# RWKV recurrence on one Trainium2 core: each head keeps one half of the partitions, and its products become pairs in diagonal quadrants

## The chip, the cores and the metric

One core of a Trainium2 chip runs the kernel, a whole network of four layers on 256 tokens of width 1024. The metric is device time in microseconds (us). The engines are TensorE (PE in the views; its weight loads are PEld), VectorE (DVE), ScalarE (ACT), GpSimd (POOL) and SyncE (SP).

## What is computed

The four layers have three kinds of mixer: RWKV (layers 0 and 3), a selective state space (layer 1), attention in a sliding window (layer 2); feed-forward blocks stand around them. The change concerns RWKV. There, 16 heads of 64 each keep a 64x64 state, which is carried over the tokens:

```python
    def step(state, inp):
        r_t, w_t, k_t, v_t, kk_t, a_t = inp
        sa = jnp.einsum('bhvk,bhk->bhv', state, -kk_t)
        state = (state * w_t[:, :, None, :]
                 + sa[..., None] * (kk_t * a_t)[:, :, None, :]
                 + v_t[..., None] * k_t[:, :, None, :])
        return state, jnp.einsum('bhvk,bhk->bhv', state, r_t)

    _, y = lax.scan(step, state0, (tm(rh), tm(wh), tm(kh), tm(vh), tm(kk), tm(ah)))
```

Then y is normalised by head, a bonus `sum(r k r_k) v` is added, and the sum is multiplied by a gate and projected by `w_o`. Inputs and results are fp32.

## The kernel before

Activations lie transposed: 1024 channels are 8 tiles k of 128 partitions, each with 256 tokens along the free axis. A tile holds two heads, one in partitions 0 to 63 and one in 64 to 127 (`H2` is the pair of slices).

The recurrence is computed in 4 chunks c of 64 tokens. Within a chunk the dependence between tokens is a triangular system: its block products L (`pd`, L832) go to DRAM and come back with one 32x32 block in a partition (`dL`, then `LT`), are inverted there by 31 steps on VectorE (`solve`, L866 and L867), and go back by DRAM (`dTU`) into `U` and `T11`. `inverse` (L948, L953) completes the 64x64 inverses from the 32x32 blocks by small products. What remains for each chunk and tile is `recur`: 

- p1 (L1008, L1011): state times decayed directions, plus the masked products `GM` times the values; ScalarE copies it to r1.
- p3 (L1016): the inverse U times r1; ScalarE copies it into UV.
- p4 (L1021): the new state out of keys and values, one product of 128 rows with [K|Aa] as weights; VectorE scales it into ST (L1026, L1028), once for each head.
- py (L1033, L1035): the chunk's output.

Where things lie: of tiles 0 to 3 the solved rows (U, r1, the upper part of UV) are in the upper half of the partitions, of tiles 4 to 7 in the lower half (`half = k // 4`), for both heads of a tile side by side along the free axis; the values are in the other half. So p4 sums over keys times values and directions times solved rows in a single product of 128 rows. `AK` keeps K and Aa side by side for that, by chunk. The state of two heads, ST, is a 128x128 tile whose off-diagonal blocks are zero.

The stages of one RWKV layer: projections and low-rank products; then for pairs of tiles `directions`, `decay`, `factors` (which makes pd), with `grams` (L933, masked on VectorE by L934) and `tokens` (four transposes, L965) of tiles 0 to 3; then `solve` with the values' projection (`whole`, L694) beside it; then the stage in which four lanes run `inverse` and `recur`, lane n for tiles n and n+4, with `grams`, `tokens`, `bonus` (L986), `inverse` of tiles 4 to 7, the rest of `whole`, and `close` (L1050 normalisation, `pgt` gate) woven between them. The output projection `pjrwo` (`mm3`, L381 to L383) follows, from Y in the order of k.

The generators are woven turn by turn into one program, and a scheduler in the framework then places the instructions on each engine, so the order is not that of the code. On an engine instructions run in their order. A pool tag "q" of QB buffers holds r1 and old; the mamba layer borrows one for its `Bt`.

An fp32 product is one instruction in the order of the program and two passes in the trace; an fp32r product is one pass. `mm` writes PSUM; `pc` is one PSUM tile for each tile k.

Of the kernel before, what the change touches and what calls it, by code (L numbers as in the profile page):

```python
# [23 lines left out]
QB = 8  # L24
# [226 lines left out]
class Net:  # L251
# [400 lines left out]
    def rwkv(self, l, j):  # L652
# [106 lines left out]


        AK = [self.b8("AK", F32, (P, 4, 4, 2, 64)) for _ in range(2)]
        Aa = lambda k, n=1: AK[k // 4][:, k % 4:k % 4 + n, :, k // 4].rearrange("p k c t -> p (k c) t")
        K = lambda k, n=1: AK[k // 4][:, k % 4:k % 4 + n, :, 1 - k // 4].rearrange("p k c t -> p (k c) t")
        keys = project(1, xk, lambda i, ps: act(K(i), c8(ps), AF.Copy))
# [9 lines left out]
        dL = self.dp.tile([2, 4, KT, 2, 32, 32], F32, name=f"dL_{l}")  # L774
# [4 lines left out]
        def directions(k0):  # L779

            sq = b2("sq")
            for d in range(2):
                act(c8(pair(sq)[:, d]), K(k0 + d), AF.Square, scale=self.p(f"k_k{j}", k0 + d))
            yield
            ss = self.ax("ss")
            mm(ss, blk, sq, start=True, stop=True)
            act(sq, ss, AF.Relu, bias=self.eps[:, 2:3])
            act(sq, sq, AF.Ln, bias=self.eps[:, 3:4])
            act(sq, sq, AF.Exp, scale=-0.5)
            for d in range(2):  # L790
                V.scalar_tensor_tensor(c8(KK[:, k0 + d]), K(k0 + d), self.p(f"k_k{j}", k0 + d), c8(pair(sq)[:, d]), MUL, MUL)
            yield
# [21 lines left out]
        def factors(k0):  # L814
            ks = range(k0, k0 + 2)
            sl = slice(k0, k0 + 2)
            kt_, a_, ip, kk = K(k0, 2), Aa(k0, 2), c8(flat(IP[:, sl])), c8(flat(KK[:, sl]))
            ka = b2("ka")
            for d, k in enumerate(ks):
                act(c8(pair(ka)[:, d]), Aa(k), AF.Identity, scale=self.p(f"k_a{j}", k), bias=rest[:, k:k + 1])  # L820
            V.tensor_tensor(a_, a_, kk, MUL)
            V.tensor_tensor(a_, a_, ip, MUL)
            V.tensor_tensor(kt_, kt_, c8(ka), MUL)
# [4 lines left out]
            for d, k in enumerate(ks):  # L828
                for c in range(4):
                    f = slice(64 * c, 64 * c + 64)  # L830
                    for r in H2:
                        mm(pd[r, 256 * d + 64 * c:256 * d + 64 * c + 64], Aa(k)[r, c], SG[r, k, f], start=True, stop=True)  # L832
# [11 lines left out]
        def solve():  # L844
# [56 lines left out]
        lows, ups = [lora_wa(lwa)], [lora_up("wa2", (j,), P, lwa, [(H2[0], f"w0{j}", lambda k: c8(SG[:, k])), (H2[1], f"a0{j}", Aa)])]  # L901
# [10 lines left out]
        received, solved, ready, U, GMs, UVs, bos = set(), [], set(), [], {}, {}, {}  # L912
# [9 lines left out]
        gm = bc(C["gm"][:, None, :], [P, 4, P])  # L922

        def grams(k):

            while k not in received or k not in factored:
                yield
            if k // 2 not in GMs:
                GMs[k // 2] = self.b8("GM", F32, (P, 2, 8, P))
            for h_, r in enumerate(H2):  # L930
                pg = self.ax("pg")
                for c in range(4):
                    mm(pg[:, P * c:P * c + P], AK[k // 4][r, k % 4, c].rearrange("p q t -> p (q t)"), SR[r, :, k, 64 * c:64 * c + 64], start=True, stop=True)  # L933
                V.tensor_tensor(GMs[k // 2][:, k % 2, 4 * h_:4 * h_ + 4], pg.rearrange("p (u t) -> p u t", t=P), gm, MUL)  # L934
                yield

        ahead = lambda k0: chain(directions(k0), decay(k0), factors(k0))
        def inverse(k):
# [3 lines left out]
            p0, n = 64 * (k // 4), 2 * (k % 4)  # L942
            a, b = slice(p0, p0 + 32), slice(p0 + 32, p0 + 64)
            GM = GMs[k // 2][:, k % 2]
            at = lambda u: 8 * (u % 4) + n + u // 4
            px, x = self.ax("px"), self.b1("X2")
            for u in range(8):
                mm(px[b, 32 * u:32 * u + 32], GM[a, u, 32:64], U[1][a, at(u)], start=True, stop=True)  # L948
            act(x[b], px[b, :256], AF.Copy)
            yield  # L950
            pt = self.ax("pt")
            for u in range(8):
                mm(pt[a, 32 * u:32 * u + 32], x[b, 32 * u:32 * u + 32], U[0][b, at(u), 32:], start=True, stop=True)  # L953
            act(U[0][a].rearrange("p (c g) t -> p c g t", g=8)[:, :, n:n + 2, 32:], pt[a, :256].rearrange("p (h c t) -> p c h t", c=4, h=2), AF.Copy)
            ready.add(k)
            yield

        def tokens(k):

            rk = self.b1("rk")  # L960
            V.scalar_tensor_tensor(c8(rk), c8(R[:, k]), self.p(f"r_k{j}", k), K(k), MUL, MUL)
            pt = self.ax("tok")
            both = AK[k // 4][:, k % 4].rearrange("p c q t -> p (c q t)")
            for c in range(4):
                nc.tensor.transpose(pt[:, P * c:P * c + P], both[:, P * c:P * c + P], ident)  # L965
            act(both, pt, AF.Copy)
# [8 lines left out]
        def bonus(k):  # L975

            half = k // 4
            top, bot = H2[half], H2[1 - half]
            while k not in valued:
                yield  # L980
            if half not in UVs:
# [846 lines left out]
```

## Time and profile before

| what | value |
|---|---|
| runs (us) | 3042.39, 3039.34, 3040.65 |
| median | 3040.65 |
| profiled execution, its own time | 3042.72 |
| its span in the profile | 3040.9 |
| PE busy | 2907.3 (96%) |
| DVE busy | 2176.8 (72%) |
| ACT busy | 1557.4 (51%) |
| stage of the recurrence, layer 0 | 358.20 to 494.30 in the span |
| stage of the recurrence, layer 3 | 2163.00 to 2304.30 in the span |

The profiled execution lies 2.07 us above the median, and 1.82 us of its time lie outside its span. A stage of the recurrence is taken here from the first product that needs the solved blocks (px, L948) to the last product of `recur` (L1033, L1035).

### The profile page before, as it was taken

The numbers are of one execution on the slowest core, as the hardware profiler recorded it, in microseconds if no ns is written. First come the engines' busy times: TensorE is split into PE (matmuls) and PEld (weight loads), VectorE is DVE, ScalarE is ACT, GpSimd is POOL, SyncE is SP. The second block draws the span as 40 slices with busy tenths as digits, with TensorE's granted clock in tenths as the row PEclk, the third lists the DMA queues.
The fourth block names the chain that finished last, engine by engine and source line by source line (L and its number), as shares of the span: only waits on it lengthen the run. The fifth ranks groups of instructions, "written<-read, shape, count | busy, mean of one in ns | idle before, by whom it ended". The sixth has DMA issues, their size and how long they took to land. (4 is left out here: it accounts for less than half of the span.)

```text
span 3040.9 us, 57272 instructions
## 1 busy us (share of the span) xinstructions
PE 2907.3 (96%) x23002; PEld 2740.7 (90%) x23002; DVE 2176.8 (72%) x3805; ACT 1557.4 (51%) x2713; POOL 88.9 (3%) x115
## 2 busy tenths in 40 slices
PE   7999899999998999999999999999899999999998
PEld 6997678999997989999988999987778999889898
DVE  8886434888787888878887888775526757566754
ACT  5446234545556765455575445445234546644543
POOL 0001200000001100000000000002100000000000
PEclk9999888999999999999999999999878999999999
DMA  9983313797874547888945887853404665544564
GB/s 320 329 312 92 117 36 112 266 308 261 292 268 151 163 154 226 289 281 280 317 132 163 304 305 253 297 173 96 127 18 125 208 181 179 177 144 125 160 184 129
DMA packets 184220, 612.33 MB, mean 201 GB/s; under 512 B 30929, under 2 KB 33361, under 8 KB 183954
## 3 DMA queue, kind: packets, MB, share of 16 engines
q1 hardware_dynamic: 168626, 595.49, 60.0%
q0 software_dynamic: 3744, 9.24, 1.0%
q10 hardware_dynamic: 11584, 3.93, 0.6%
q8 instruction: 180, 2.95, 0.4%
q14 instruction: 86, 0.70, 0.1%
HBM read 603.31 MB, written 5.28 MB: 200 GB/s over the span
## 5 line engine op out<-in xcount | busy, mean ns | idle before, releaser
L294 ACT ACTIVATE wh<-raw 128x1024 fp32r<-128x1024 f32 (+3 forms) x824 | 851.1, 1036 | 955.5 <-DMA raw<-in_wi 286.5
L373 DVE TENSOR_TENSOR wl<-raw,wh 128x1024 fp32r<-128x1024 f32 (+3 forms) x824 | 987.3, 1200 | 400.5 <-ACT wh L294 393.0
L382 PE MATMUL pjwi<-xl,wh 128*128 128x256 f32 x2568 | 720.8, 282 | 4.5 <-DVE xl L506 4.1
L383 PE MATMUL pjwi<-xh,wl 128*128 128x256 f32 x2568 | 717.4, 281 | 0.0
L381 PE MATMUL pjwi<-xh,wh 128*128 128x256 f32 x2568 | 714.5, 282 | 2.2 <-ACT sa L294 1.3
L382 PEld LDWEIGHTS pjwi<-xl,wh 128*128 128x128 f32 x2568 | 484.3, 189 | 7.2 <-DVE xl L506 6.9
L383 PEld LDWEIGHTS pjwi<-xh,wl 128*128 128x128 f32 x2568 | 483.3, 189 | 0.0
L381 PEld LDWEIGHTS pjwi<-xh,wh 128*128 128x128 f32 x2568 | 480.7, 189 | 2.8 <-ACT sa L294 1.6
L382 PE MATMUL pdwo<-gl,wh 128*128 128x256 f32 x1408 | 395.7, 281 | 0.0
L383 PE MATMUL pdwo<-gh,wl 128*128 128x256 f32 x1408 | 394.9, 280 | 0.0
L381 PE MATMUL pdwo<-gh,wh 128*128 128x256 f32 x1408 | 394.8, 280 | 0.0
L422 DVE SCALAR_TENSOR_TENSOR aring<-aring,cbc 128x1024 f32<-128x1024 f32 x286 | 343.5, 1219 | 4.1 <-DMA aring<-in_adaw 4.1
L383 PEld LDWEIGHTS pdwo<-gh,wl 128*128 128x128 f32 x1408 | 265.4, 188 | 0.0
L381 PEld LDWEIGHTS pdwo<-gh,wh 128*128 128x128 f32 x1408 | 265.1, 188 | 0.0
L382 PEld LDWEIGHTS pdwo<-gl,wh 128*128 128x128 f32 x1408 | 265.1, 188 | 0.0
L694 PE MATMUL whole<-mf,raw 128*128 128x256 f32 x512 | 127.0, 403 | 1.4 <-DMA raw<-in_rkv 1.4
L694 PEld LDWEIGHTS whole<-mf,raw 128*128 128x128 f32 x512 | 100.8, 201 | 22.6 <-issue 5.7
L383 PE MATMUL pjw2i<-xh,wl 128*128 128x256 f32 x416 | 119.0, 286 | 0.0
L381 PE MATMUL pjw2i<-xh,wh 128*128 128x256 f32 x416 | 118.5, 285 | 0.0
L382 PE MATMUL pjw2i<-xl,wh 128*128 128x256 f32 x416 | 117.9, 284 | 0.0
L381 PE MATMUL pjmbi<-xh,wh 128*128 128x256 f32 x352 | 101.1, 291 | 7.4 <-DVE cv L1152 4.9
L382 PE MATMUL pjmbi<-xl,wh 128*128 128x256 f32 x352 | 102.0, 291 | 0.1
(528 smaller groups left out, 5743.8 us busy)
## 6 DMA issues: line engine op xcount, KB each, us to landing
raw<-in_wi SPq DMA_DIRECT2D x352, 512.0 KB, 4.7
aring<-in_adaw SPq DMA_DIRECT2D x286, 512.0 KB, 5.4
raw<-in_wo SPq DMA_DIRECT2D x128, 512.0 KB, 4.8
raw<-in_w2i SPq DMA_DIRECT2D x56, 512.0 KB, 4.0
raw<-in_wo SPq DMA_DIRECT2D x64, 384.0 KB, 4.4
raw<-in_rkv SPq DMA_DIRECT2D x48, 512.0 KB, 3.7
raw<-in_mbi SPq DMA_DIRECT2D x48, 512.0 KB, 3.7
raw<-in_fg SPq DMA_DIRECT2D x22, 512.0 KB, 3.8
```

The costliest lines, as they stand in the source:

```text
L294: ins = self.nc.scalar.activation(out, in_, func, **k)
L373: self.last = self.nc.vector.tensor_tensor(lo, src, hi.bitcast(F32), SUB)
L381: mm(out, a, xh[:parts, k, :], start=start, stop=False)
L382: mm(out, a, xl[:parts, k, :], start=False, stop=False)
L383: mm(out, b, xh[:parts, k, :], start=False, stop=stop)
L422: ins = nc.vector.scalar_tensor_tensor(raw, raw, 1.0, self.cbc, MUL, MUL, accum_out=m[:, b % 24:b % 24 + 1])
L694: mm(ps[:, :T], w[:, k * P:k * P + P], x[0][:, k, :], start=k == 0, stop=k == KT - 1)
```

## The change

Each head stays in its own half of the partitions throughout. K and Aa become plain tiles; the values, transposed, go into `Vt`, the solved rows into `uu`, each head's 64 rows in its half. Every product of `recur` becomes a pair: 64x64 weights and 64 moving columns for the head in the upper half, the same for the lower one (`both`). What was one product of 128 rows for p4 is now two pairs that add up in PSUM, and the output gets a third pair (`uu` by `MB`), as p1 and py lose the rows of the other half. The state is one tile of 128x64, so that VectorE scales it in one instruction and no zeros are kept.

`grams` makes K against both directions (`pk`, masked into LM), and Aa against R alone (`pa`, masked into MB); Aa against the directions, which it had made again, is now kept from pd as LL and used in `inverse`. `tokens` and `bonus` transpose head by head, by products with a 64x64 block of the identity or of `cen`. `inverse` takes a pair of tiles at a time, both heads in two strips of rows. Four DMAs a pair of tiles write dL in place of eight; `solve` loads LT when all 8 tiles are there, where it loaded a half after 4. `recur` also waits until Vt is written (`prepared`). In the mamba layer Bt moves to a tile of its own, since "q" buffers are now 128x64 and 16 in number.

```diff
-QB = 8
+QB = 16
...
-        AK = [self.b8("AK", F32, (P, 4, 4, 2, 64)) for _ in range(2)]
...
+        K, Aa = self.b8("K"), self.b8("Aa")
+        LL = self.b8("LL")
...
-            tm = b2("tm")
-            act(tm, pd, AF.Copy)
+            act(flat(LL[:, sl]), pd, AF.Copy)
             for n in range(4):
                 h_, i = divmod(n, 2)
-                for d, k in enumerate(ks):
-                    queues[(n + d) % 2].dma_start(dL[k // 4, :, 2 * (k % 4) + h_, i].rearrange("c s t -> s c t"),
-                                                  c8(pair(tm)[32 * n:32 * n + 32, d])[:, :, 32 * i:32 * i + 32])
+                queues[n % 2].dma_start(dL[h_, k0:k0 + 2, :, i].rearrange("k c s t -> s (k c) t"),
+                                        c8(flat(LL[32 * n:32 * n + 32, sl]))[:, :, 32 * i:32 * i + 32])
...
-            for half in range(2):
-                while len(factored) < 4 * half + 4:
-                    yield
-                queues[half].dma_start(L[64 * half:64 * half + 64], dL[half].rearrange("c g i s t -> (c g i) (s t)"))
+            while len(factored) < KT:
+                yield
+            for h_ in range(2):
+                queues[h_].dma_start(L[64 * h_:64 * h_ + 64], dL[h_].rearrange("k c i s t -> (k c i) (s t)"))
...
-            for h_, r in enumerate(H2):
-                pg = self.ax("pg")
+            pa, pk = self.ax("pa"), self.ax("pk")
+            for c in range(4):
+                f = slice(64 * c, 64 * c + 64)
+                for r in H2:
+                    mm(pk[r, P * c:P * c + P], K[r, k, f], SR[r, :, k, f], start=True, stop=True)
+            V.tensor_tensor(LM[k // 4][:, k % 4], pk.rearrange("p (c t) -> p c t", c=4), bc(C["gm"][:, None, :], [P, 4, P]), MUL)
+            yield
+            for c in range(4):
+                f = slice(64 * c, 64 * c + 64)
+                for r in H2:
+                    mm(pa[r, f], Aa[r, k, f], R[r, k, f], start=True, stop=True)
+            V.tensor_tensor(c8(MB[0][:, k]), c8(pa[:, :T]), bc(C["gm"][:, None, 64:], [P, 4, 64]), MUL)
...
+            for n, u in xs:
+                k, c = divmod(u, 4)
+                for a, b in zip(lo, hi):
+                    mm(px[b, 32 * n:32 * n + 32], LL[a, k, 64 * c + 32:64 * c + 64], U[1][a, u], start=True, stop=True)
+            for b in hi:
+                act(x[b], px[b, :256], AF.Copy)
...
-                nc.tensor.transpose(pt[:, P * c:P * c + P], both[:, P * c:P * c + P], ident)
-            act(both, pt, AF.Copy)
+                    f = slice(64 * c, 64 * c + 64)
+                    for r in H2:
+                        mm(pt[r, o + 64 * c:o + 64 * c + 64], src[r, k, f], ident[r, r], start=True, stop=True)
+            for o, src in ((0, Aa), (T, K)):
+                act(src[:, k], pt[:, o:o + T], AF.Copy)
...
+            both = lambda out, w, x, **k: [mm(out[r], w[r], x[r], **k) for r in H2]
+            q1 = lambda name: self.sp.tile([P, 64], F32, tag="q", name=name, bufs=QB)
...
+                both(p1, lm[:, c, :64], V_[:, k, f], start=True, stop=not c)
                 if c:
-                    mm(p1, SR[:, 0, k, f], st, start=True, stop=False)
-
-                for h_ in range(2):
-                    mm(hc(p1, h_), GM[:, 4 * h_ + c, :64], uv(h_), start=not c, stop=not c or h_ == 1)
+                    both(p1, SR[:, 0, k, f], st, start=False, stop=True)
                 r1 = q1("r1")
-                act(r1[top], p1, AF.Copy)
-                yield
-                for h_ in range(2):
-                    mm(hc(p3, h_), U[0][top, 8 * c + n + h_], hc(r1[top], h_), start=True, stop=True)
-                act(UV[top, P * c:P * c + P], p3, AF.Copy)
+                act(r1, p1, AF.Copy)
+                yield
+                both(p3, U[0][:, 4 * k + c], r1, start=True, stop=True)
+                uu = q1("uu")
+                act(uu, p3, AF.Copy)
...
-                    mm(p4, both[:, P * c:P * c + P], UV[:, P * c:P * c + P], start=True, stop=True)
...
+                    both(p4, K[:, k, f], V_[:, k, f], start=True, stop=False)
+                    both(p4, Aa[:, k, f], uu, start=False, stop=True)
+                    new = q1("st")
...
-                for h_, r in enumerate(H2):
-                    mm(py[r, f], uv(h_), GM[:, 4 * h_ + c, 64:], start=True, stop=not c)
+                both(py[:, f], V_[:, k, f], lm[:, c, 64:], start=True, stop=False)
                 if c:
-                    mm(py[:, f], st, SR[:, 1, k, f], start=False, stop=True)
+                    both(py[:, f], st, SR[:, 1, k, f], start=False, stop=False)
+                both(py[:, f], uu, MB[0][:, k, f], start=False, stop=True)
...
-        lanes = [chain(repeat(None, s), inverse(n), recur(n, sts(n)), recur(n + 4, sts(n))) for n, s in enumerate(STAGGER)]
+        lanes = [chain(repeat(None, s), recur(n), recur(n + 4)) for n, s in enumerate(STAGGER)]
...
-        weave(lanes + [rs, chain(*(chain(grams(k), tokens(k), bonus(k), inverse(k)) for k in range(4, KT)))] + [closing(k) for k in range(0, KT, 2)] + [splits()])
+        rest = chain(*(chain(grams(k), tokens(k), bonus(k)) for k in range(4, KT)))
+        weave([chain(*(inverse(k0) for k0 in range(0, KT, 2)))] + lanes + [rs, rest] + [closing(k) for k in range(0, KT, 2)] + [splits()])
```

How the instructions stand on the engines: the first place is the recurrence on TensorE in layer 0, while four lanes are under way. A row has the line, the operation, output and inputs, the shape of the weights or of the output, and how many stand one behind the other. Before, with p1 (L1008, L1011), p3 (L1016), p4 (L1021) and py (L1033, L1035):

```order
L1033 MATMUL pc<-GM,UV 64x64 x2
L1035 MATMUL pc<-SR,ST 128x64
L1008 MATMUL pc<-ST,SR 64x128
L1011 MATMUL pc<-UV,GM 64x64 x2
L1021 MATMUL pc<-UV,AK 128x128
```

After the change every pair has the line of `both`, L1009; `LM,Vt`, `SR,st` and `MB,uu` are py, `Vt,LM` and `st,SR` p1, `r,U` p3:

```order
L1009 MATMUL pc<-LM,Vt 64x64 x2
L1009 MATMUL pc<-SR,st 64x64 x2
L1009 MATMUL pc<-MB,uu 64x64 x2
L1009 MATMUL pc<-Vt,LM 64x64 x2
L1009 MATMUL pc<-st,SR 64x64 x2
...
L938 MATMUL pa<-SR,Aa 64x64 x8
L1009 MATMUL pc<-Vt,LM 64x64 x4
L1009 MATMUL pc<-r_4377,U 64x64 x2
L1009 MATMUL pc<-r_4383,U 64x64 x2
L975 MATMUL tok<-cbase,Aa 64x64 x8
```

Five shapes in a chunk have become one, and the two products of a pair stand next to each other. The second place is the end of the same stage on TensorE, where the output projection pjrwo already runs between the last products of the recurrence. Before:

```order
L383 MATMUL pjrwo<-yh,wl 128x256
L381 MATMUL pjrwo<-yh,wh 128x256
L382 MATMUL pjrwo<-yl,wh 128x256
L1033 MATMUL pc<-GM,UV 64x64 x2
L1035 MATMUL pc<-SR,ST 128x64
L1008 MATMUL pc<-ST,SR 64x128
L1011 MATMUL pc<-UV,GM 64x64 x2
...
L1016 MATMUL pc<-r_4493,U 64x64 x2
```

After the change:

```order
L383 MATMUL pgt<-lgs,wl 128x256
L1009 MATMUL pc<-r_4876,U 64x64 x2
L381 MATMUL pjrwo<-yh,wh 128x256
L382 MATMUL pjrwo<-yl,wh 128x256
L383 MATMUL pjrwo<-yh,wl 128x256
L1009 MATMUL pc<-Vt,K 64x64 x2
L1009 MATMUL pc<-uu,Aa 64x64 x2
```

The first pjrwo now stands where the last chunk's p3 does; 13 of them are ahead of the last product of the recurrence, where 54 were. The third place is VectorE at the beginning and at the end of `solve` in layer 0. Before:

```order
L934 TENSOR_TENSOR GM<-pg,crw 128x512
L866 TENSOR_TENSOR fs<-LT 128x31
...
L373 TENSOR_TENSOR wl<-raw,wh 128x1024
L866 TENSOR_TENSOR fs<-LT 128x31
L867 TENSOR_TENSOR LT<-LT,fs 128x31
L870 COPY LT<-LT 128x1024
```

After the change:

```order
L939 TENSOR_TENSOR MB<-pa,crw 128x256
L913 TENSOR_TENSOR SR<-SR,whole 128x256
L969 SCALAR_TENSOR_TENSOR rk<-SR,par,K 128x256
L861 TENSOR_TENSOR fs<-LT 128x31
...
L861 TENSOR_TENSOR fs<-LT 128x31
L862 TENSOR_TENSOR LT<-LT,fs 128x31
L865 COPY LT<-LT 128x1024
L373 TENSOR_TENSOR wl<-raw,wh 128x1024
```

Ahead of the first step of solve now stand the last R product (L913) and rk (L969) of tile 3; wl, the split of a loaded gate weight, has moved behind the COPY that ends solve.

## Rows read from the trace of the kernel before

**Rows 1.** The page: busy times, and granted clock in 40 slices.
```profile
PE 2907.3 (96%) x23002; PEld 2740.7 (90%) x23002; DVE 2176.8 (72%) x3805; ACT 1557.4 (51%) x2713; POOL 88.9 (3%) x115
PEclk9999888999999999999999999999878999999999
```
**Rows 2.** By stretch: us, PE PEld DVE ACT POOL busy, PEclk, DMA share, GB/s.
```profile
358.20:494.30 136.10, 136.10 (x1048) 107.70 (x1048) 37.73 (x93) 47.27 (x133) 0.87 (x1) 0.80 0.10 30
2163.00:2304.30 141.30, 139.94 (x1048) 111.17 (x1048) 37.74 (x93) 47.53 (x134) 3.37 (x3) 0.77 0.12 34
```
**Rows 3.** Timeline of PE, one chunk; start, us, instruction.
```profile
408.08 0.34 PE L1033 MATMUL pc<-GM,UV 128*64 128x64 f32 x4
408.35 0.43 PE L1035 MATMUL pc<-SR,ST 128*128 128x64 f32 x2
408.71 0.44 PE L1016 MATMUL pc<-r,U 64*64 64x64 f32 x4
409.09 0.43 PE L1008 MATMUL pc<-ST,SR 128*64 128x128 f32 x2
409.36 0.39 PE L1011 MATMUL pc<-UV,GM 128*64 128x64 f32 x4
409.68 0.49 PE L1021 MATMUL pc<-UV,AK 128*128 128x128 f32 x2
410.10 0.44 PE L1016 MATMUL pc<-r,U 64*64 64x64 f32 x4
```
**Rows 4.** Timeline of PE: whole, grams, small inverses, output projection.
```profile
281.67 5.78 PE L694 MATMUL whole<-mf,raw 128*128 128x256 f32 x26
...
400.89 1.16 PE L933 MATMUL pg<-SR,AK 64*128 64x128 f32 x8
401.97 0.49 PE L1021 MATMUL pc<-UV,AK 128*128 128x128 f32 x2
...
413.97 0.69 PE L948 MATMUL px<-T,GM 32*32 32x32 f32 x16
...
505.87 0.28 PE L383 MATMUL pjrwo<-yh,wl 128*128 128x256 f32 x1
505.99 0.28 PE L381 MATMUL pjrwo<-yh,wh 128*128 128x256 f32 x1
```
**Rows 5.** Products in diagonal quadrants: timeline of PE, then durations (min/median/max ns).
```profile
305.07 1.15 PE L832 MATMUL pd<-SR,AK 64*64 64x64 f32 x32
306.15 1.71 PE L933 MATMUL pg<-SR,AK 64*128 64x128 f32 x16
...
L832 PE MATMUL pd<-SR,AK x256: 218/218/267, 279.2 to 2113.5; 64*64 64x64 f32 x128
```
**Rows 6.** By stretch within the recurrence, layers 0 and 3; columns as rows 2.
```profile
410.00:420.00 10.00, 10.00 (x119) 8.51 (x118) 2.04 (x6) 5.26 (x18) 0.00 (x0) 1.00 0.01 2
460.00:480.00 20.00, 20.00 (x110) 14.90 (x107) 5.00 (x14) 6.12 (x17) 0.00 (x0) 0.50 0.01 4
2260.00:2290.00 30.00, 30.00 (x162) 22.66 (x161) 5.96 (x16) 8.47 (x24) 0.00 (x0) 0.50 0.05 14
```
**Rows 7.** ScalarE's copies of tile pc by shape: min/median/max ns.
```profile
L294 ACT ACTIVATE r<-pc x30: 252/272/274, 378.0 to 492.1; 64x128 f32<-64x128 f32 x30
```
**Rows 8.** Timelines of DVE, ACT's queue and PE, from pd to inverse, layer 0.
```profile
301.58 0.41 DVE L918 TENSOR_TENSOR SR<-SR,whole 128x256 f32<-128x256 f32 x1
306.89 1.77 ACTq L839 DMA_DIRECT2D dL<-tm  x4
316.28 0.19 DVE L866 TENSOR_TENSOR fs<-LT 128x31 f32<-128x31 f32 x1 [0.27 <-DMA LT<-dL]
344.85 1.22 DVE L373 TENSOR_TENSOR wl<-raw,wh 128x1024 fp32r<-128x1024 f32 x1
346.43 1.04 DVE L870 COPY LT<-LT 128x1024 f32<-128x1024 f32 x1
358.16 1.03 PE L948 MATMUL px<-T,GM 32*32 32x32 f32 x16 [9.49 <-DMA T<-dTU]
```

More of the change, by code (lines that the diff above doesn't have):

```diff
@@ L927, in grams @@
                 yield
-            if k // 2 not in GMs:
-                GMs[k // 2] = self.b8("GM", F32, (P, 2, 8, P))
-            for h_, r in enumerate(H2):
-                pg = self.ax("pg")
-                for c in range(4):
-                    mm(pg[:, P * c:P * c + P], AK[k // 4][r, k % 4, c].rearrange("p q t -> p (q t)"), SR[r, :, k, 64 * c:64 * c + 64], start=True, stop=True)
-                V.tensor_tensor(GMs[k // 2][:, k % 2, 4 * h_:4 * h_ + 4], pg.rearrange("p (u t) -> p u t", t=P), gm, MUL)
-                yield
+            if not MB:
+                MB.append(self.b8("MB"))
@@ L950, in inverse @@
             yield
             pt = self.ax("pt")
[L952 to L955, printed above, removed]
+            for n, u in xs:
+                for a, b in zip(lo, hi):
+                    mm(pt[a, 32 * n:32 * n + 32], x[b, 32 * n:32 * n + 32], U[0][b, u, 32:], start=True, stop=True)
@@ L956, in inverse @@
+            for a in lo:
+                act(U[0][a, 4 * k0:4 * k0 + 8, 32:], pt[a, :256].rearrange("p (u t) -> p u t", t=32), AF.Copy)
+            ready.update((k0, k0 + 1))
             yield
@@ L975, in bonus, with recur @@
         def bonus(k):
-            half = k // 4
-            top, bot = H2[half], H2[1 - half]
             while k not in valued:
                 yield
-            if half not in UVs:
-                UVs[half] = self.b8("UV", F32, (P, 4, 512))
-                nc.gpsimd.memset(UVs[half][top], 0.0)
+            if not Vt:
+                Vt.append(self.b8("Vt"))
             pv = self.ax("tokv")
             for c in range(4):
-                mm(pv[bot, P * c:P * c + P], Vv[:, k, 64 * c:64 * c + 64], C["cen"], start=True, stop=True)
-            act(UVs[half][bot, k % 4], pv[bot], AF.Copy)
+                f = slice(64 * c, 64 * c + 64)
+                for r in H2:
+                    mm(pv[r, f], Vv[r, k, f], C["cen"][r, r], start=True, stop=True)
+            act(Vt[0][:, k], pv[:, :T], AF.Copy)
             V.tensor_tensor(Vv[:, k], bos.pop(k), Vv[:, k], MUL)
+            prepared.add(k)
             yield
-        def recur(k, sts):
-            while k not in ready:
+        def recur(k):
+            while k not in ready or k not in prepared:
                 yield
-            half, n = k // 4, 2 * (k % 4)
-            top = H2[half]
-            GM = GMs[k // 2][:, k % 2]
-            UV = UVs[half][:, k % 4]
-            both = AK[half][:, k % 4].rearrange("p c q t -> p (c q t)")
             pc = self.mm("pc")
+            p1, p3, p4 = (pc[:, 64 * i:64 * i + 64] for i in range(3))
             py = pys[k] = pc[:, 256:]
-            q1 = lambda name: self.sp.tile([P, P], F32, tag="q", name=name, bufs=QB)
+            both = lambda out, w, x, **k: [mm(out[r], w[r], x[r], **k) for r in H2]
+            q1 = lambda name: self.sp.tile([P, 64], F32, tag="q", name=name, bufs=QB)
+            lm, V_ = LM[k // 4][:, k % 4], Vt[0]
             st = old = None
```

65 lines of the change are left out of this document (27 added, 38 removed).

## Prediction

> **What bounds the kernel now.** I read the page first. TensorE is busy for 96% of the span, and the granted clock, full almost everywhere, falls in two places of the 40 slices [rows 1]: both are RWKV layers. Then I took busy times by stretch, from the first product that needs the solved blocks to the last product of `recur`, in both layers. The reader is to see that TensorE is busy for the whole of either stretch but 1.36 us, while VectorE and ScalarE are at a third of it, and that the clock is at 0.80 and 0.77 of full [rows 2]. So this stage lasts as long as TensorE's work at the clock that it is granted: 136.10 x 0.80 = 108.9 and 141.30 x 0.77 = 108.8 us at full clock. The same work in both layers comes out the same, which is a check on this way of reading. What the change is worth is decided here, by that work, by the clock, and by whether TensorE still never waits.
>
> Third, the timeline of TensorE gives prices at full clock, from one start to the next. One chunk of one tile runs from 408.08 to 410.10, 2.02 us [rows 3]. The first chunk of a tile lacks the two products with the state (0.36 and 0.27), the last one p4 (0.42): 4 x 2.02 - 1.05 = 7.03, and 8 tiles make 56.2. A pass of `whole` costs 5.78 / 26 = 0.222, a gram pass (401.97 - 400.89) / 8 = 0.135, 16 passes of a small inverse 0.69, a pass of pjrwo 0.12 [rows 4].
>
> As a check, the stage before from these prices: recurrence 56.2; 64 passes of `whole` 14.2; 64 of grams 8.6; 16 groups of small inverses 11.0; 48 passes for `tokens` and `bonus`, at pjrwo's price, 5.8; 36 of pgt and 54 of pjrwo 10.8; bonus sums (8 passes of 256 columns) 1.8; normalisation (8 of 512) 3.5. That is 111.9 against the 108.9 shown, 3% too much.
>
> **The pairs.** The trace of before holds products of just the new form: pd multiplies 64x64 blocks for the upper and the lower head in turn, in diagonal quadrants, into one PSUM tile. Its 32 passes take 1.15 us, the last alone 0.218, so passes come every (1.15 - 0.218) / 31 = 0.030 us [rows 5]. The 4 passes of p3, which are 64x64 in a single quadrant, take 0.38 to the next start [rows 3]. The next shape after pd starts 1.08 after pd does, 0.12 later than 32 x 0.030: that is what a change of shape costs. Without it a p3 pass takes 0.065. So a pair (4 passes) costs 0.12 us in the new form, and 0.26 if its halves do not run side by side.
>
> That two quadrants may write one PSUM tile at once is what a rule speaks against. The Trainium skill, page "TensorEngine Tiling (Array Packing)", section "Gotcha 1: PSUM Pressure", says that different row tiles write to different PSUM banks and cannot use the same bank at once; by that, all pairs of this change would take turns, which is the third rival below. The trace disagrees: pd's halves write one tile at 0.030 us a pass.
>
> **The sum for the stage, at full clock.** A tile has 6 pairs in the first chunk, 8 in each of the next two, 6 in the last, so 28; 8 tiles have 224, at 0.12: 26.9. `whole` 14.2, bonus sums 1.8, normalisation 3.5, pgt 4.3 stay. Grams: pk has 64 passes of 128 columns, taken at twice 0.030: 3.8; pa 64 at 0.030: 1.9. `tokens` becomes 128 passes (it had 16 of full width): 3.8. `bonus` 64: 1.9. The small inverses keep their 256 passes, now alternating between two strips; 11.0 if that gives nothing, 5.5 if it halves them as it does for quadrants; I take 7, nearer to the pairs' row. Changes of shape that are left: 58 in this stretch of the new order, where 178 stood; 58 x 0.12 = 7.0 (before, those of the recurrence are inside its 2.02). Only 13 passes of pjrwo stand ahead of the last product of the recurrence: 1.6. Sum 77.7. The 41 passes that leave the stage have not gone; they are run behind it, 41 x 0.12 = 4.9. So 82.6 us in place of 108.9.
>
> **The clock.** The stretch from 410 to 420, with recurrence of four lanes, ran at 1.00; 460 to 480, and 2260 to 2290, at 0.50, TensorE being busy all the time [rows 6]. These are the two levels, 2.4 and 1.2 GHz. In the slow stretches short products that fill a part of the array change shape from one to the next. The new stage has a third of these changes, and both heads' quadrants at work. I therefore expect full clock after the beginning. There, 16 passes of px took 1.03 behind an idle time of 9.49 us [rows 8], and 0.69 later [rows 4]; that wait for DMA remains, so some us at the lower level remain. I take a mean of 0.95, with 0.77 and 1.00 as ends: 82.6 / 0.95 = 87.
>
> **Waits.** Before, there were so many us of work in a chunk that the lanes always found their r1, uu and state ready. Now a tile has 11 points at which a pair needs what ScalarE or VectorE has just written (3 in each of three chunks, 2 in the last), 88 in all. ScalarE's copy takes 0.27 [rows 7]; the state's scaling, one instruction in place of two, I price the same. If nothing covered any of them TensorE would wait 88 x 0.27 = 24 us; if other lanes, `whole` and pgt cover all, none. The order puts pairs of two lanes behind each other and other work between, yet in the second place shown three passes of pjrwo (0.36) are all that stands between p3 and the p4 that needs its result. I take a third, 8 us. So the stage takes 95 us, and gives 136.1 - 95 = 41 and 141.3 - 95 = 46: 87 us.
>
> **Ahead of the stage.** The chain here is pd, dL and LT by DMA, 31 steps on VectorE, dTU and U by DMA. ScalarE issued four dL writes for the last pair in 1.77 us, now two: -0.9. LT was awaited last for the half that came last, so that both now wait for all 8 tiles costs nothing. VectorE has the last R product and rk ahead of the first step of solve (0.41 each, both 128x256): +0.8. The split of a gate weight, 1.22 us, stood ahead of solve's last step and the COPY, and is now behind [rows 8]: -1.2, unless the loaded weight is late anyway. Together about -1 in a layer; ends +2 (no DMA gain, and the R product late) and -3. Bt in its own tile changes nothing that the mamba stage waits for; the memsets of ST and UV were on GpSimd, off the path.
>
> Sum: 3042.7 - 87 - 2 = 2953.7 for the profiled execution, which lies 2.07 above the median; so 2951.
>
> **Rivals.**
> The clock stays low. For it: this stage still has short products, and the tail between pgt and pjrwo. Against: the full clock of 410 to 420. At 0.80 and 0.77 the work takes 103.3 and 107.3; with 4 us of waits (slower products cover more) the gain is 136.1 - 107.3 + 141.3 - 111.3 = 59, and the time 3042.7 - 59 - 2 - 2 = 2980. Chance 0.15.
>
> The waits come through. Nothing covers them, 24 us instead of 8: the stage takes 111, the gain is 55, the time 2984. For it: VectorE's and ScalarE's queues also hold masks and copies of other tiles ahead of a lane's. Against: four lanes in turn. Chance 0.08.
>
> The halves of a pair take turns, and the kernel is slower. pd's 32 products were independent of each other and nothing was added up in PSUM; here pairs accumulate onto one another. At 0.065 a pass: recurrence 896 passes x 0.035 = +31.4; pa, `tokens`, `bonus` 256 x 0.035 = +9.0; pk at the gram price 0.135, 64 x 0.075 = +4.8; inverses +4. That is 82.6 + 49.2 = 131.8, above the 108.9 of before; at 0.80 and 0.77 it lasts 164.8 and 171.2, 59 longer than before in sum: 3042.7 + 59 - 2 - 2 = 3098. It decides from the point at which 26.3 of the 49.2 us are lost, when a pair costs 0.12 + 0.53 x 0.14 = 0.19 us. Against it stands the row of pd. Chance 0.04.
>
> That the scheduler tears the pairs apart is excluded by the order: the two stand next to each other.
>
> **Chances and range.** My forecast has 0.73. Lowest: full clock, no waits, 82.6 us, gain 112, time 2926; highest of the forecast's kind: both rivals' prices or an inverse that gains nothing (+4 in each layer on 2984), 2992. So 2925 to 2995, which leaves out the slower rival and mixtures. About 0.2%, 6 us, is what a measurement of this kernel can tell from no change; faster by more has 0.95, no change 0.01, slower 0.04.
>
> **What would show it.** In the new profile: pairs at 0.12 us in the timeline of TensorE; a clock near 1 in the two slices; TensorE idle for some 8 us in the stage, behind ScalarE's r1 and uu; the stage 95 us long. A pair at 0.2 or more, a stage with clock 0.5, or idle time above 20 us would make me wrong, each in the way of its rival.

## The result, and the profile after

The changed kernel took 2914.3 us in the median of 4 runs (2910.04 to 2923.34), the kernel before 3041.5 (3039.34 to 3048.27, 4 runs): a ratio of 0.9582, with a 95% interval from 0.9555 to 0.9609, or 127 us less. I had forecast 2951 and a range from 2925 to 2995, so the direction was right and the size too small; the time lies below the range. The profiled execution of the changed kernel took 2923.34, 9.0 more than its median, with a span of 2921.6, 119.3 less than before. The steps are measured against that span.

The page, busy times and granted clock by slices:

```profile
PE 2806.9 (96%) x24570; PEld 2672.8 (91%) x24570; DVE 2160.3 (74%) x3757; ACT 1537.8 (53%) x2729; POOL 72.3 (2%) x93
PEclk9999999999999999999999999999999999999899
```

The two dips of [rows 1] are gone; the one near the end lies in a feed-forward block that the change does not touch. Busy times of the same stage as in [rows 2], then of stretches within it as in [rows 6] (us, busy PE, PEld, DVE, ACT and POOL, granted clock, DMA share, GB/s):

```profile
346.05:432.20 86.15, 82.11 (x1600) 68.34 (x1601) 30.08 (x70) 40.50 (x143) 1.12 (x2) 0.96 0.23 71
2101.94:2188.90 86.96, 82.55 (x1587) 68.43 (x1585) 29.99 (x70) 39.35 (x140) 0.00 (x0) 0.96 0.25 74
...
346.00:356.00 10.00, 6.97 (x57) 5.53 (x58) 1.21 (x1) 2.53 (x7) 1.12 (x2) 0.66 0.67 167
356.00:376.00 20.00, 19.86 (x466) 16.82 (x467) 5.60 (x14) 11.16 (x36) 0.00 (x0) 1.00 0.31 108
396.00:416.00 20.00, 19.77 (x373) 15.66 (x370) 9.64 (x24) 11.45 (x41) 0.00 (x0) 1.00 0.01 2
```

The stage went from 136.10 and 141.30 to 86.15 and 86.96: 104.3 us of the 119.3. TensorE's work in it is 82.11 x 0.96 = 78.8 and 82.55 x 0.96 = 79.2 us at full clock, where it was 108.9. Below full clock are only the first 10 us, behind the wait for the solved blocks. TensorE's timeline shows the prices (start, us, instruction):

```profile
302.18 1.09 PE L932 MATMUL pk<-SR,K 64*64 64x128 f32 x16
303.10 0.63 PE L938 MATMUL pa<-SR,Aa 64*64 64x64 f32 x16
303.57 0.63 PE L975 MATMUL tok<-cbase,Aa 64*64 64x64 f32 x16
...
367.08 0.69 PE L953 MATMUL px<-T,LL 32*32 32x32 f32 x32
367.70 0.33 PE L1009 MATMUL pc<-Vt,LM 64*64 64x64 f32 x4
...
370.08 0.28 PE L1009 MATMUL pc<-Vt,K 64*64 64x64 f32 x4
370.19 0.28 PE L1009 MATMUL pc<-uu,Aa 64*64 64x64 f32 x4
```

A pair (4 passes) starts 0.11 to 0.12 us behind the one ahead of it. 32 passes of a small inverse last 0.69, as 16 did [rows 4], and take 0.62 to the next start: the two strips overlap like the quadrants do. 16 gram passes of 128 columns take 0.92, 16 of 64 columns 0.47.

For what TensorE waited in the stage of layer 0, then of layer 3 (us in total, times, longest):

```profile
PE whole L694 <- DMA raw<-in_rkv: 2.5, 1, 2.5
PE px L953 <- DMA T<-dTU: 1.9, 2, 1.4
PE pc L1009 <- DVE st L1031: 0.6, 2, 0.3
PE pc L1009 <- ACT y L294: 0.2, 1, 0.2
...
PE px L953 <- DMA T<-dTU: 2.4, 1, 2.4
PE pc L1009 <- DVE Vv L885: 1.0, 1, 1.0
PE pc L1009 <- DVE st L1031: 0.5, 1, 0.5
...
2101.68 0.33 PE L1009 MATMUL pc<-Vt,LM 64*64 64x64 f32 x4 [1.02 <-DVE Vv L885]
```

The last line, from TensorE's timeline, is the wait for Vv: it ends at 2101.68, ahead of the first px of layer 3 (2101.94), so it lies ahead of the stage. That for y is for a PSUM tile that ScalarE had to read out first. Of 88 points in a layer at which a pair needs what another engine has just written, the profile shows a wait at two in layer 0 (0.6 us together) and at one in layer 3 (0.5).

And ahead of the stage: VectorE from the start of solve to its end, then TensorE's first product that needs the solved blocks (idle time and what ended it in brackets), which answer to [rows 8].

```profile
310.11 0.42 DVE L913 TENSOR_TENSOR SR<-SR,whole 128x256 f32<-128x256 f32 x1 [2.72 <-PE whole L694]
310.97 0.18 DVE L861 TENSOR_TENSOR fs<-LT 128x31 f32<-128x31 f32 x1
332.39 0.42 DVE L998 TENSOR_TENSOR Vv<-rk,Vv 128x256 f32<-128x256 f32 x1 [0.56 <-DMA vf<-Vv]
337.17 1.07 DVE L865 COPY LT<-LT 128x1024 f32<-128x1024 f32 x1
...
346.05 0.22 PE L953 MATMUL px<-T,LL 32*32 32x32 f32 x2 [1.44 <-DMA T<-dTU]
```

px comes at 346.05 and not at 358.16, and TensorE was idle ahead of it for 1.44 us, not 9.49. Counted from the first product of the preparation (ss) in its layer, px comes 11.4 us earlier in layer 0 and 8.8 in layer 3. I had put 1 there.

So of the span's 119.3 us, 104.3 come from the stage and 20.2 from ahead of it; 3.4 are given back behind it, where the passes of pjrwo now stand (from the stage's end to the last pjrwo 4.3 more in layer 0, 0.9 less in layer 3), and the rest of the network takes 1.8 longer.

### The profile page after: what moved, and what is told of

It is laid out like the page before. It is cut to its first block, busy times and chain, and to the rows that moved or that the text cites. A ratio compares the mean times of both kernels' runs of the same rounds, so it can differ in the third digit from the quotient of the medians.

```text
span 2921.6 us, 60335 instructions
## 1 busy us (share of the span) xinstructions
PE 2806.9 (96%) x24570; PEld 2672.8 (91%) x24570; DVE 2160.3 (74%) x3757; ACT 1537.8 (53%) x2729; POOL 72.3 (2%) x93
```

## The experiments

### What the pairs cost

First, whether halves that run side by side are what made the stage short. The products of p1, p4 and py were sorted by half:

```diff
+            def apart(*ps):
+                for r in H2:
+                    for n, (out, w, x) in enumerate(ps):
+                        mm(out[r], w[r], x[r], start=n == 0, stop=n == len(ps) - 1)
...
-                both(p1, lm[:, c, :64], V_[:, k, f], start=True, stop=not c)
-                if c:
-                    both(p1, SR[:, 0, k, f], st, start=False, stop=True)
+                apart((p1, lm[:, c, :64], V_[:, k, f]), *([(p1, SR[:, 0, k, f], st)] if c else []))
...
```

> The changed kernel with the halves of its pairs pulled apart: in p1, p4 and py all products of the upper head come first, then all of the lower one (runs of two or three), p3 stays a pair. The same products, the same shapes. Theory A (the stage gains since the two halves run side by side): the other half can begin only with the last pass of a run, so a run of n products costs (2n-1) x 0.059 us in place of n x 0.059; per tile 7 groups of two pairs cost 0.12 more each and 3 groups of three 0.24 more: 1.5 us a tile, 12 a layer, 24 in all at full clock, so about 2938, and the pass in a run at 0.059 us in the timeline. Rival (the gain comes from fewer changes of shape and the clock, the halves' overlap is small change): within 6 us of the changed kernel, 2914. Rival (the clock is granted by how full the array is): the clock in the stage falls too, towards 0.8, and the time is 2960 or more.

It took 2920.9 us (ratio to before 0.9611, 0.9584 to 0.9637); the stage was 3.6 us longer in layer 0 and 1.8 in layer 3, and its clock no lower:

```profile
343.40:433.10 89.70, 85.41 (x1600) 71.88 (x1601) 30.11 (x70) 39.74 (x143) 1.12 (x2) 0.96 0.22 70
```

That is far from theory A's 2938 and close to the rival's 2914: 6.6 above the changed kernel by the medians, with intervals that overlap. The probe, in the same set of runs, says which part of theory A was wrong. It adds these products, which nothing uses:

```diff
+            cases = (("alt1", [top, bot] * 16, 1), ("alt2", [top, bot] * 16, 2), ("one", [top] * 32, 1), ("three", [top, top, top, bot, bot, bot] * 5, 1))
...
+                    mm(o[r, g:g + 64], blk[r, r], K[r, 7, g:g + 64], start=True, stop=True)
```

> The changed kernel with four blocks of unused products added after the recurrence of layer 0, 64x64 weights and 64 columns each: 32 that alternate between the halves into one PSUM tile (alt, the first), 32 that alternate into two PSUM tiles (alt, the second), 32 of the upper half alone (one), 30 in runs of three (three). Theory A (halves run side by side whatever the tile they write): 64 passes of either alt take 64 x 0.0295 = 1.9 us, one 64 x 0.059 = 3.8, three 10 runs of 5 x 0.059 = 2.95. Rival (halves that write one PSUM tile take turns): the first alt 3.8, the second 1.9, three 3.5 or more. Rival (no overlap, each pass of 64 columns costs 0.03 wherever it stands once nothing depends on it): all about 1.9.

TensorE's timeline has the two alternating blocks as one group of 128 passes:

```profile
441.52 3.95 PE L1124 MATMUL alt<-K,cbase 64*64 64x64 f32 x128
445.30 3.89 PE L1124 MATMUL one<-K,cbase 64*64 64x64 f32 x64
449.03 2.08 PE L1124 MATMUL three<-K,cbase 64*64 64x64 f32 x60
451.04 0.38 PE L383 MATMUL pjrwo<-yh,wl 128*128 128x256 f32 x1
```

128 passes take 3.78 us to the next start, 0.0295 each, in one PSUM tile and in two alike: had the first 64 taken turns, the group would have lasted 3.8 + 1.9. The 64 in one half take 3.73, 0.058 each. So halves do overlap, and one PSUM tile is no hindrance. Runs of three, though, take 2.01 for 60 passes, 0.0335 each: a run of that length still overlaps with the run of the other half behind it. My picture that the other half begins only with the last pass of a run was wrong, and with it the 12 us a layer that I had expected of the first run. That run therefore does not test the overlap; a longer separation does.

In the next kernel a lane runs all chunks of its tile's upper head, then all of the lower one:

```diff
-            both = lambda out, w, x, **k: [mm(out[r], w[r], x[r], **k) for r in H2]
+            both = lambda out, w, x, **k: mm(out[r], w[r], x[r], **k)
...
-                act(r1, p1, AF.Copy)
+                act(r1[r], p1[r], AF.Copy)
...
-        lanes = [chain(repeat(None, s), recur(n), recur(n + 4)) for n, s in enumerate(STAGGER)]
+        lanes = [chain(repeat(None, s), recur(n, 0), recur(n, 1), recur(n + 4, 0), recur(n + 4, 1)) for n, s in enumerate(STAGGER)]
```

> The changed kernel with the two heads of a tile one after the other: each of the four lanes runs the recurrence of its tile's upper head, then that of the lower one, so that neighbouring products of the recurrence are all in one half. The same products in number and shape; ScalarE and VectorE get twice as many instructions, on 64 partitions each. Theory A (the halves' overlap is worth its half of the time; runs of three were too short to lose it): 896 passes of the recurrence at 0.058 us in place of 0.029, +26 us in a layer at full clock, the stage of layer 0 at 112 us or more in place of 86, both together 2966 or more, and 2990 if the clock falls to 0.9 with it or the copies make TensorE wait. Rival (what counts is that shapes no longer change): the stage stays within 6 us, the time under 2930.

It took 3012.8 us (0.9916, 0.9898 to 0.9933): 98 of the 127 us were gone. By stretch, the stage in both layers and two stretches within it:

```profile
350.40:476.20 125.80, 123.60 (x1579) 108.45 (x1579) 33.21 (x87) 57.19 (x220) 1.12 (x2) 0.78 0.14 47
2139.20:2262.80 123.60, 120.44 (x1572) 105.75 (x1570) 33.12 (x87) 56.47 (x218) 0.02 (x1) 0.82 0.17 52
...
380.00:400.00 20.00, 20.00 (x347) 17.84 (x346) 8.00 (x17) 7.92 (x34) 0.00 (x0) 1.00 0.31 108
440.00:460.00 20.00, 20.00 (x195) 19.85 (x194) 2.59 (x10) 8.37 (x38) 0.00 (x0) 0.50 0.01 1
```

TensorE's work is 123.60 x 0.78 = 96.4 and 120.44 x 0.82 = 98.8 us at full clock, 18 and 20 more than in the changed kernel (26 were expected; that lanes which have got to different halves still overlap may be the reason, but was not traced). The rest is the clock, which falls to its lower level in the second half of the stage, as it did before the change [rows 6], although TensorE is busy for 20.00 of 20.00 us there. From 380 to 400, where passes of `whole` and grams stand between the products of one half, it was still at 1.00; from 440 to 446 the timeline shows nothing but products of the recurrence. That run has each copy and scaling of the recurrence in two instructions (220 on ScalarE in the stage in place of 143), and its products no longer come in pairs, so it needs a control. The same kernel, with two of the four lanes beginning with the lower head:

```diff
...
-        lanes = [chain(repeat(None, s), recur(n, 0), recur(n, 1), recur(n + 4, 0), recur(n + 4, 1)) for n, s in enumerate(STAGGER)]
+        lanes = [chain(repeat(None, s), recur(n, n % 2), recur(n, 1 - n % 2), recur(n + 4, n % 2), recur(n + 4, 1 - n % 2)) for n, s in enumerate(STAGGER)]
```

> As the run with the two heads of a tile one after the other, but two of the four lanes begin with the lower head: at any time two lanes work in the upper half and two in the lower. The same instructions on all engines as in that run, only which half comes when. Theory A (the time and the clock were lost since neighbouring products were all in one half): the halves overlap again between lanes, the clock in the stage is back above 0.95, the stage takes 86 to 95 us, the time 2915 to 2935. Rival (they were lost by the doubled number of instructions on ScalarE and VectorE, or by products that no longer stand in pairs): near 3013 again.

```profile
347.60:448.00 100.40, 96.98 (x1582) 80.21 (x1583) 35.34 (x88) 62.26 (x220) 1.12 (x2) 0.97 0.19 61
2112.30:2215.00 102.70, 98.78 (x1576) 81.31 (x1574) 35.12 (x88) 61.34 (x217) 0.00 (x0) 0.93 0.21 62
```

2951.4 us (0.9715, 0.9689 to 0.9741). With the same instructions on each engine, 61 us came back by nothing but which half a lane begins with. The clock is at 0.97 and 0.93 again; in layer 3 it still falls twice for some us (0.70 from 2182 to 2187, 0.68 from 2192 to 2197). The work, 94.1 and 91.9 us, is only 2 and 7 less than with the halves apart: lanes overlap each other's halves now and then, not as closely as pairs do. Of the range that I had given for theory A (2915 to 2935) it misses the upper end by 16; that the overlap is looser is the likely reason. So two things are told apart here. Most of the difference between the two kernels is the clock, which was kept where both halves had work at any time: of the 56.7 us between their profiled executions 46.3 lie in the two stages, of which only 9 are work, and the rest behind the stages, where the clock of the run with its halves apart is still at its lower level for some us. And the 37 us from there to the changed kernel (2951.4 - 2914.3) are what close pairs and undivided copies are worth together, 15.3 and 12.7 of work in the two stages among them; TensorE's idle time in the stage, 3.4 and 3.9 us, is no longer than in the changed kernel, so the copies do not show as waits.

Of the 30 us by which TensorE's work in a stage fell (108.9 to 79), the halves apart give back 18 to 20. The other 10 to 12 (fewer changes of shape, passes of pjrwo that left the stage, cheaper grams) are priced in the prediction, but no run takes them singly.

### What came earlier ahead of the stage

The first step of solve, its COPY and px are traced against the first ss of the layer. VALUES, 2 in both kernels, is the number of tiles whose values are projected ahead of solve. The table has starts from the timelines of the profiled executions, in us behind that ss, for layers 0 and 3; the times are medians:

| kernel | last pd | first step | COPY | px | time (us), ratio to before |
|---|---|---|---|---|---|
| before | 33.7, 34.0 | 44.9, 44.8 | 75.0, 76.2 | 86.8, 85.8 | 3041.5 |
| changed | 27.6, 29.2 | 40.3, 41.6 | 66.5, 69.2 | 75.4, 77.0 | 2914.3, 0.9582 |
| before, 4 writes of dL | 31.2, 32.5 | 42.1, 43.3 | 70.7, 75.1 | 86.0, 84.8 | 3035.2, 0.9980 |
| changed, 8 writes of dL | 28.1, 29.4 | 41.1, 40.8 | 66.7, 68.4 | 75.3, 76.3 | 2921.5, 0.9611 |
| changed, pd by a shared buffer | 33.2, 33.6 | 43.6, 42.9 | 69.2, 69.7 | 79.0, 77.1 | 2913.5, 0.9590 |
| before, bonus behind the values | 33.6, 33.8 | 44.9, 44.7 | 69.2, 71.2 | 84.9, 81.1 | 3034.0, 0.9985 |
| changed, VALUES = 1 | 28.1, 28.5 | 38.6, 38.0 | 63.8, 65.7 | 75.3, 76.0 | 2916.5, 0.9598 |
| changed, VALUES = 0 | 29.4, 29.5 | 38.5, 40.0 | 64.4, 66.6 | 76.4, 77.9 | 2909.9, 0.9576 |

The changed kernel gains 4.6 and 3.2 us up to the first step, 3.9 and 3.8 (75.0 - 44.9 against 66.5 - 40.3, and so on) within solve, and 2.9 and 1.8 from COPY to px.

The number of DMA writes of dL, done alone in the kernel before (with the rows of LT in another order, so that one write can take two tiles) and undone alone in the changed one:

```diff
-                for d, k in enumerate(ks):
-                    queues[(n + d) % 2].dma_start(dL[k // 4, :, 2 * (k % 4) + h_, i].rearrange("c s t -> s c t"),
-                                                  c8(pair(tm)[32 * n:32 * n + 32, d])[:, :, 32 * i:32 * i + 32])
+                queues[n % 2].dma_start(dL[k0 // 4, h_, k0 % 4:k0 % 4 + 2, :, i].rearrange("k c s t -> s (k c) t"),
+                                        c8(tm[32 * n:32 * n + 32])[:, :, 32 * i:32 * i + 32])
...
```

> The kernel before with one part of the change alone: dL is written by 4 DMAs for a pair of tiles in place of 8 (the rows of LT in another order, so that two tiles join). Theory B (what the change gained ahead of the recurrence, 6 us at the last pd, comes from fewer DMA issues on the queues of ScalarE and GpSimd): the last pd of layer 0 comes 4 to 6 us earlier than at 305.07, px 4 to 9 us earlier than 358.16, both layers together 8 to 16 us: 3026 to 3033. Rival (it comes from the buffers: the copy of pd no longer takes one of the three 128x512 buffers that sq, cs and ka use): the two waits for dL<-tm of 0.7 and 0.8 us shrink a little at most, 0 to 3 us in all, 3038 to 3041. Rival (it comes from the scheduler's other order on VectorE and TensorE): no change, 3041.

> The changed kernel with 8 DMA writes of dL for a pair of tiles, as before, in place of 4. Theory B (fewer issues): the last pd of layer 0 comes 4 to 6 us later than at 298.20, px likewise, both layers 8 to 14 us, 2922 to 2928. Rival (buffers, or the order): px within 2 us, 2914 to 2917.

In the kernel before, fewer writes bring the last pd and the first step 1.5 to 2.8 us forward, less than theory B's 4 to 6, and px only 0.8 and 1.0: in layer 0, where COPY comes 4.3 earlier, 3.5 of it are waited for behind COPY. In the changed kernel more writes cost no more than 0.8 us at any mark, and px nothing. Its median is 7 us above the changed kernel's, within the two intervals, and no mark of these layers shows them. Theory B falls as the main cause.

The buffer: pd through one of the three 128x512 buffers again; LL gets a second copy by ScalarE, behind the writes of dL.

```diff
-            act(flat(LL[:, sl]), pd, AF.Copy)
+            tm = b2("tm")
+            act(tm, pd, AF.Copy)
...
+            act(flat(LL[:, sl]), pd, AF.Copy)
```

> The changed kernel with pd copied into one of the three 128x512 buffers that sq, cs and ka use too, as before, and dL written from there (by 4 DMAs); LL gets a copy of its own after that. Theory C (what came earlier ahead of the recurrence came from that buffer being free: the next pair of tiles waits until dL has been read out of it): in the order 55 passes of whole stand ahead of the last pd again, not 42; last pd 31 to 34 us behind the first ss in place of 27.6, px 80 us or more behind it in place of 75.4; 5 to 10 us a layer, 2924 to 2934. Rival (other parts of the new order): within 3 us of the changed kernel at both marks.

Its last pd is back at 33.2 and 33.6, as theory C said: between the first ss and the last pd of layer 0 stand 55 products of `whole` again (110 passes in the trace, 84 in the changed kernel), and TensorE reaches it later. So the buffer, with that second copy, accounts for the earlier pd. But the first step loses only 3.3 and 1.3, px 3.6 and 0.1, and the time nothing: 2913.5. So theory C explains the mark and not the time.

Last of the four theories, the waits of bonus within solve. In the kernel before, VectorE waits there for 3.7 us in layer 0 and 3.6 in layer 3 (the two longest of layer 0 below), in the changed kernel for 0.6 and not at all:

```profile
322.22 0.43 DVE L988 TENSOR_TENSOR Vv<-rk,Vv 128x256 f32<-128x256 f32 x1 [1.22 <-PE tokv L986]
333.46 0.43 DVE L988 TENSOR_TENSOR Vv<-rk,Vv 128x256 f32<-128x256 f32 x1 [1.62 <-DMA vf<-Vv]
```

They were taken out of the kernel before:

```diff
-        weave([solve(), fill, gates(), chain(*(bonus(k) for k in range(4)))])
+        weave([solve(), chain(fill, *(bonus(k) for k in range(4))), gates()])
```

> The kernel before with bonus of tiles 0 to 3 behind the values' projection, no longer woven in beside solve. In the kernel before, four instructions of bonus (L988) stand between the steps of solve on VectorE and wait there for 3.7 us in layer 0; the changed kernel has 0.6 of such waits. Theory D (these waits are part of what the change gained ahead of the recurrence): solve, from its first step to COPY, takes 26 to 28 us in place of 30.2 in layer 0, px comes 2 to 4 us earlier against the first ss, and the time is 3033 to 3038. Rival (the DMA behind solve, or the work that now stands behind px, takes it back): px or the time unchanged, 3040.

```profile
315.45 0.19 DVE L866 TENSOR_TENSOR fs<-LT 128x31 f32<-128x31 f32 x1 [0.35 <-DMA LT<-dL]
339.70 1.06 DVE L870 COPY LT<-LT 128x1024 f32<-128x1024 f32 x1
...
355.46 1.03 PE L948 MATMUL px<-T,GM 32*32 32x32 f32 x16 [11.50 <-DMA T<-dTU]
```

solve takes 24.3 and 26.5 us in place of 30.2 and 31.3, more than expected; px comes 1.9 and 4.7 earlier, and the time is 3034.0 against 3038.1 of the kernel before in these runs (0.9985, 0.9970 to 1.0001): as theory D had it in size, though the interval just reaches no change. So VectorE's waits and the work between solve's steps are what solve can be shortened by, and with 3.1 and 3.6 us fewer of such waits they account for most of the changed kernel's 3.9 and 3.8 there; that this made the time shorter is not shown. In layer 0 the stretch from COPY to px took 15.8 us in place of 11.7, 11.5 of it a wait for DMA, and took most of it back.

The profiled executions of both edits of the kernel before lie 9 and 11 us above their medians: their stages of layer 0 took 142.9 and 142.4 us at a clock of 0.75 and 0.77, in place of 136.1 at 0.80. This differs by more than the gains that are looked for here, so the marks ahead of the stage say more than the times.

Finally, whether the rest can be had by shortening the chain further, with VALUES = 1 and 0 in the changed kernel.

> The changed kernel with the values of one tile, not two, projected ahead of solve (VALUES = 1); the other goes beside it. In the profile of the changed kernel VectorE waits 2.7 us for the R product of tile 3 just ahead of the first step of solve. If that wait is on the path: first step 2 to 3 us earlier against the first ss, px the same, 4 to 6 us in both layers, 2908 to 2911. If TensorE's passes of whole, which all stand ahead of px, or the DMA behind solve set px: no change, 2914.

> As the run with VALUES = 1, with no values projected ahead of solve. By the order only 35 passes of whole stand ahead of the last pd. If that path sets px: 3 to 6 us in a layer, 2902 to 2908; otherwise no change, or some us more where bonus waits for its values while solve runs, 2914 to 2920.

The first step comes 1.6 to 3.6 us earlier, COPY 2.1 to 3.5, and px at the same place: 75.3 to 77.9 in all six. Up to px TensorE is busy for this long (kernel before, changed kernel, VALUES = 0, layer 0; then px with VALUES = 0, for which TensorE does not wait):

```profile
271.40:358.20 86.80, 73.30 (x494) 58.48 (x493) 57.70 (x127) 35.34 (x70) 28.43 (x38) 0.96 0.46 132
...
270.60:346.00 75.40, 72.07 (x685) 57.71 (x684) 56.13 (x126) 31.54 (x70) 20.01 (x25) 1.00 0.43 125
...
267.90:344.30 76.40, 72.81 (x690) 58.55 (x688) 54.69 (x126) 32.37 (x70) 19.27 (x24) 1.00 0.43 126
...
344.31 0.69 PE L953 MATMUL px<-T,LL 32*32 32x32 f32 x32
```

72 to 73 us of work stand ahead of px on TensorE in each of these. With 86.8 us from ss to px there was room to gain some 13 by a shorter chain; the changed kernel has used 11 of it, and with either value of VALUES px comes when TensorE gets to it. This is why a chain that is 2 to 4 us shorter up to COPY leaves the time where it is. Of the four edits in the changed kernel only the shared buffer moves px by more than 1 us (3.6 in layer 0, a wait for DMA of 4.6), which an interval of 6 us to either side does not resolve. None of them is shown to beat it: VALUES = 0 is at 0.9576 (0.9560 to 0.9592) against 0.9582 (0.9555 to 0.9609).

## Why the prediction was right or wrong

**The pairs, right.** 0.12 us was forecast for a pair from the rows of pd, and 0.11 to 0.12 is what the timeline shows. The sum for the stage was 77.7 us at full clock; TensorE did 78.8 and 79.2. The small inverses (7 taken, 5.5 as the lower bound) came out at 8 x 0.62 = 5.0.

**The clock, right in size, its reason only in part.** Mean 0.95 was taken, 0.96 measured, low only behind the wait for DMA. I named changes of shape and a partly filled array together as the reason. With equal shapes throughout the recurrence and the halves apart the clock fell all the same, and with the halves mixed it came back to 0.97 and 0.93; so which halves are at work is enough to decide most of it in this stage. Whether changes of shape do anything by themselves was not tried.

**Waits, mis-sized.** The step "I take a third, 8 us" failed: 0.8 and 0.7 us in the two layers were waited for VectorE and ScalarE in the recurrence, of 24 if nothing had covered them. Four lanes in pairs cover nearly all. TensorE's idle time in the stage is 4.0 and 4.4 us, but most of it is for DMA at the start (the solved blocks, and the weights of `whole`, which TensorE now asks for earlier). The stage and what it leaves behind it come to 90.5 and 86.1, where 95 was the sum: 13 us of the miss in both layers. Half of that is the stage's idle time. The other half lies behind the stage, most of it in layer 3: the 41 passes of pjrwo that moved there were priced at 4.9, which layer 0 bears out (4.3); in layer 3 TensorE had stood idle there for 2.7 us at a mean clock of 0.87, and in the changed kernel it neither waits nor slows down, which took the price back (from the stage's end to the last pjrwo, before, then after; columns as in [rows 2]).

```profile
2304.30:2329.60 25.30, 22.59 (x154) 21.30 (x155) 17.27 (x29) 14.19 (x24) 0.00 (x0) 0.87 0.64 200
...
2188.90:2213.30 24.40, 24.40 (x195) 23.37 (x196) 17.75 (x31) 15.10 (x26) 0.00 (x0) 1.00 0.63 216
```

**Ahead of the stage, mis-sized.** "Together about -1 in a layer; ends +2 and -3" failed, with 11.4 and 8.8: 18 us of the miss. I counted what I saw move in the order at the two ends of solve. What I left out: VectorE's waits for bonus inside solve, which the trace of before shows and I gave no price, 3.7 and 3.6 us, of which 0.6 and none are left; that pd comes earlier once its copy does not hold a shared buffer (the order showed 42 products of `whole` ahead of it in place of 55), which moves the mark of pd, though its part in the time is not shown; and the bound on the other side, TensorE's 73 us up to px against 86.8, which says that as much as 13 could be gained. Which of these made px come earlier, and by how much, stays open: no single edit brings the kernel before to the changed one's px. Why the stretch from COPY to px took 2.9 and 1.8 us less is open too; it differs between 7.5 and 15.8 us from kernel to kernel.

**The rivals.** The clock that stays low and the pairs that take turns did not come. The kernel with its halves apart has both in part, for another reason than the rival's: neighbouring products there stand in one half, whereas halves that write one PSUM tile do overlap in the probe. The waits did not come.

**The range.** Its lower end took no waits and full clock for the stage, but let the chain ahead of it gain 2 us in all: 2928.7 for a profiled execution, where 2923.3 was measured. The chain gained 18 more than that; the stage with what lies behind it, 11.4 longer in both layers than at that end, and 1.8 in the rest of the network took 13 of it back. Another 7 us lie beside the sum, which is made for one execution: that of the changed kernel was 9.0 above its median, that of before 2.1.

## What to carry to other kernels

Price products in quadrants by alternation: 64x64 blocks of two heads that stand in diagonal quadrants cost half, if products of both halves keep coming within a few instructions of each other, and here that also kept TensorE's clock up. Where a chain of waits stands ahead of a stage, give two numbers before pricing single moves: how long the chain is, and how much work the bounding engine has up to that point; their difference is the most that any sum of small moves can win. A wait inside a chain has a price even if the change does not name the instruction: the scheduler moves it.

## What the runs showed of the hardware

- Two quadrants that write one PSUM tile run side by side as if they wrote two: 0.0295 us a pass for either. The rule in the Trainium skill (page "TensorEngine Tiling (Array Packing)", section "Gotcha 1: PSUM Pressure"), by which they could not use one PSUM bank at once, does not hold for the products of this kernel.
- The overlap does not need strict alternation: runs of three products (6 passes) still come at 0.0335 us a pass, against 0.058 in one half alone.
- TensorE's granted clock fell to the lower level, 0.50, in a stretch in which it was busy for 20.00 of 20.00 us, when its products were those of the recurrence alone and neighbours stood in one half; in the same run it was at 1.00 while `whole` and grams stood between them, and with the same instructions and both halves in use it was at 0.97 and 0.93 over the stage. So a TensorE that the profile counts as busy did not keep the clock by that alone.
- Two strips of 32x32 products overlap too: 32 passes in 0.62 us to the next start, 0.69 from first to last, which is what 16 had taken.
